# Weights' second parts made by transfers that add, in place of a VectorE subtraction, with four slots of each kind

## The chip, the core and the metric

The program runs on one core of one Trainium2 chip. The metric is the device time of one execution, in microseconds (us), and lower is better. The kernel before took 3535.98 us (median of two runs, 3535.84 and 3536.11).

## The reference

The reference is a chain of two transformer stacks on 512 tokens of width 1024, all in fp32. The first has four layers; each projects the normalised tokens (w_in, 1024 x 3328), mixes them (stick-breaking attention in layers 0 and 3, differential attention in layer 1, a short convolution in layer 2), adds an attention over 256 memory tokens (w_mem_kv), projects back (w_o) and runs a gated feed-forward of inner width 2816 (w_ffn_in, w_ffn_out). The second has one layer: a spatial gating branch and an RWKV-7 recurrence side by side, then a feed-forward of inner width 4096. Nearly all arithmetic is a product of tokens with weights:

```
proj = hn @ w_in[i]
x = x + jnp.concatenate([mix, mo], axis=-1) @ w_o[i]
gu = x @ w_in;  (silu(gu[..., :D_FF]) * gu[..., D_FF:]) @ w_out
p = a @ w_in[l];  h = h + mixed @ w_out[l]
h = h + jnp.square(jax.nn.relu(f @ w_ffn1[l])) @ w_ffn2[l]
```

## The kernel before, in words

Tokens lie along the free axis and features along the 128 partitions. To keep fp32 accuracy at the speed of the format fp32r, every operand of a large product is split into two fp32r parts, `hi` (the value rounded) and `lo` (what the rounding left). A product is then three matmuls: hi times hi, hi times lo, lo times hi (`mm3`).

Weights come in chunks of 128 x 1024 fp32 (512 KB), made by `wblk`. For each chunk:

1. SyncE loads the raw weights into a slot of the ring `wr` (line 305).
2. ScalarE casts them into a slot of the ring `wh`, the hi part.
3. VectorE subtracts wh from wr into a slot of the ring `wl`, the lo part (`sub`).
4. TensorE runs 24 matmuls of 512 columns (or 48 of 256) on wh and wl, which frees both slots.

There are 584 chunks, some 8 of them smaller than 512 KB. The rings have `WR` and `WH` slots; before, three each. A new chunk's cast can run when TensorE has done with the chunk three before it. The instructions of `wblk` have a raised priority (`WPRI`), so the scheduler of the framework puts them into each engine's order ahead of other ready work. Each engine then executes its own order strictly in sequence, so an instruction that waits holds up all that stand behind it on that engine. GpSimd (POOL) has few instructions in this kernel: it issues the transfers that aren't weight loads, such as `mx` (memory tokens, loaded back from DRAM at the end of each mixing stage by `mem_load`), and in the second stack `ar`, `bk`, `dL`, `dv`, `bv`, `gl`, `dga`, `dob` (stored) and `W`, `vv`, `x`, `c` (loaded) for the recurrence.

All other temporaries of 128 x 512 fp32 (`c`) come from one pool: `NCT` slots in the first stack, `NCT2` in the second. The recurrence (`chain`) is a side lane of eight rounds, between whose matmuls the planner puts those of weights (`ga`, `gb`, and `acc` of w_pa). Every recorded compute instruction and POOL transfer carries the line 152, that of the wrapper which records it; matmuls carry line 285.

Of the kernel before, what the change touches and what calls it, by code (L numbers as in the profile page):

```python
# [8 lines left out]
F32 = mybir.dt.float32  # L9
F32R = mybir.dt.float32r  # L10
AF = mybir.ActivationFunctionType
ALU = mybir.AluOpType
# [160 lines left out]
class Build:  # L173
# [123 lines left out]
    def wblk(self, src, kc, cols, also={}, sizes=None):  # L297

        nc = self.nc
        step = max(1, 1024 // cols)  # L300
        out, k0, rows = [], 0, src.shape[0]
        with self.tc.high_priority(offset=WPRI):
            for i, n in enumerate(sizes or [min(step, kc - k) for k in range(0, kc, step)]):
                raw = self.wp.tile([rows, n, cols], F32, tag="wr", name=self.nm("wr"), bufs=WR)
                nc.sync.dma_start(out=raw, in_=src[:, k0:k0 + n])
                also.get(i, lambda: 0)()
                hi = self.wp.tile([rows, n, cols], F32R, tag="wh", name=self.nm("wh"), bufs=WH)
                lo = self.wp.tile([rows, n, cols], F32R, tag="wl", name=self.nm("wl"), bufs=WH)
                self.untimed |= {hi.name, lo.name}
                nc.scalar.copy(hi, raw)  # L310
                self.sub(lo, raw, hi)
                out += [(hi[:, k], lo[:, k]) for k in range(n)]
                k0 += n
        return out
# [790 lines left out]
    def pools2(self, ctx):  # L1105
        ep = ctx.enter_context
        self.kp = ep(self.tc.tile_pool(name="kp2", bufs=NCT2, reuse_waits="tile"))
        self.sp = ep(self.tc.tile_pool(name="sp2", bufs=4, reuse_waits="tile"))
# [690 lines left out]
MW, DW, M0, FILL, MS = 1, 1.5, 8, (99, 1, 99), 8  # L1799
VL, KSU, ENDS = 2, "kkksksss", 1  # L1800
SPRI, SOLVE_LAT, KSL, ZSL = 200, 1.3, 2, 6
NCT2 = 31
LRL, ZB, HOLD, CY, END = 0.6, 2, 2, 0.1, 2
WR, WH, WPRI, NCT = 3, 3, 150, 37


def program(tc, nc, out, depth=DEPTH, second=True, **io):
# [40 lines left out]
```

## Time and profile before

| what | value |
|---|---|
| median of the runs | 3535.98 us |
| the profiled execution's own time | 3537.37 us |
| its span, first to last instruction | 3535.6 us |
| TensorE matmul busy | 3497.0 us (99%) |
| VectorE busy | 1930.7 us (55%) |
| ScalarE busy | 1431.8 us (40%) |
| GpSimd busy | 201.9 us (6%) |
| weight loads (queue q1) | 306.22 MB, 27.3% of 16 DMA engines |
| GpSimd's transfers (queue q0) | 68.67 MB, 7.2% |

PE is TensorE's matmul row and PEld its weight load, which overlaps it; DVE is VectorE, ACT ScalarE, POOL GpSimd, SP SyncE. A letter q behind an engine means its queue of issues. The matmuls' durations overlap because they are pipelined, so a rate is read from a count over a stretch of time and not from a mean. DMA share is the mean busy share of the core's 16 DMA engines.

### The profile page before, as it was taken

Reading aid. Unit: us, or ns where it says so; the run is one execution under the profiler, and the core shown is the slowest. Engines: PE = TensorE matmul, PEld = TensorE weight load, DVE = VectorE, ACT = ScalarE, POOL = GpSimd, SP = SyncE. Lnnn points to the kernel's source line nnn. Section 1 sums busy time; section 2 is a strip of 40 time slices with the busy share of each in tenths; the row PEclk is TensorE's granted clock in tenths of the full one; section 3 lists DMA queues with packets and bytes.
Section 4 is the critical chain, followed back from the end, with each engine's and each line's share of the span. In section 5 each row is a group of like instructions: output and inputs, shape, how many; then the busy total and the mean of one; then the engine's idle time right before and its main releaser. Section 6 shows DMA issues by size and latency. Waiting matters only on the chain. (4 is left out here: it accounts for less than half of the span.)

```text
span 3535.6 us, 43485 instructions
## 1 busy us (share of the span) xinstructions
PE 3497.0 (99%) x17462; PEld 2941.1 (83%) x17462; DVE 1930.7 (55%) x2879; ACT 1431.8 (40%) x2198; POOL 201.9 (6%) x315
## 2 busy tenths in 40 slices
PE   9999999999999999999999999999999999999998
PEld 7888888888888888888888888888878888788887
DVE  7675444577643456553446665444687645464434
ACT  6673222444432343332235663223564433443322
POOL 1000000000000000000000000000033332200000
PEclk9999999999999999999999999999999999999999
DMA  5232333323333233323332122333366665433332
GB/s 186 80 96 96 94 99 97 96 72 99 99 95 99 95 96 108 107 96 95 101 95 84 60 72 96 95 101 96 111 191 161 153 190 144 153 96 99 98 95 78
DMA packets 116139, 377.81 MB, mean 107 GB/s; under 512 B 14544, under 2 KB 23184, under 8 KB 115936
## 3 DMA queue, kind: packets, MB, share of 16 engines
q1 hardware_dynamic: 94112, 306.22, 27.3%
q0 software_dynamic: 21680, 68.67, 7.2%
q8 instruction: 137, 2.24, 0.3%
q14 instruction: 66, 0.54, 0.0%
q10 hardware_dynamic: 144, 0.13, 0.0%
HBM read 344.00 MB, written 30.93 MB: 106 GB/s over the span
## 5 line engine op out<-in xcount | busy, mean ns | idle before, releaser
L152 DVE TENSOR_TENSOR wl<-wr,wh 128x1024 fp32r<-128x1024 f32 (+2 forms) x584 | 702.5, 1205 | 929.7 <-ACT wh L152 922.7
L152 ACT CAST wh<-wr 128x1024 fp32r<-128x1024 f32 (+2 forms) x584 | 604.8, 1038 | 1210.4 <-PE acc L285 536.5
L285 PE MATMUL g<-xl,wh 128*128 128x512 f32 x704 | 273.9, 389 | 0.0
L285 PE MATMUL g<-xh,wh 128*128 128x512 f32 x704 | 273.9, 389 | 0.0
L285 PE MATMUL acc<-hid,wl 128*128 128x512 f32 x704 | 273.9, 389 | 0.0
L285 PE MATMUL u<-xh,wl 128*128 128x512 f32 x704 | 273.9, 389 | 0.0
L285 PE MATMUL u<-xh,wh 128*128 128x512 f32 x704 | 273.9, 389 | 0.0
L285 PE MATMUL u<-xl,wh 128*128 128x512 f32 x704 | 273.9, 389 | 0.0
L285 PE MATMUL acc<-hid,wh 128*128 128x512 f32 x704 | 273.9, 389 | 0.0
L285 PE MATMUL acc<-hidl,wh 128*128 128x512 f32 x704 | 273.9, 389 | 0.0
L285 PE MATMUL g<-xh,wl 128*128 128x512 f32 x704 | 273.8, 389 | 0.0
L152 ACT ACTIVATE c<-c 128x512 f32<-128x512 f32 (+1 forms) x163 | 102.3, 629 | 269.6 <-DVE c L152 268.8
L285 PE MATMUL qk<-xh,wh 128*128 128x512 f32 x448 | 180.3, 402 | 6.6 <-ACT xh L152 6.6
L285 PE MATMUL acc<-h,wh 128*128 128x512 f32 x448 | 173.3, 395 | 4.8 <-ACT h L152 3.7
L285 PE MATMUL acc<-hl,wh 128*128 128x512 f32 x448 | 176.4, 394 | 0.6 <-DVE hl L152 0.5
L285 PE MATMUL qk<-xl,wh 128*128 128x512 f32 x448 | 176.1, 393 | 0.5 <-DVE xl L152 0.5
L285 PE MATMUL qk<-xh,wl 128*128 128x512 f32 x448 | 175.8, 392 | 0.0
L285 PE MATMUL acc<-h,wl 128*128 128x512 f32 x448 | 175.4, 392 | 0.0
L285 PEld LDWEIGHTS g<-xh,wl 128*128 128x128 f32 x704 | 132.2, 188 | 27.6
L285 PEld LDWEIGHTS acc<-hidl,wh 128*128 128x128 f32 x704 | 132.1, 188 | 27.5
L285 PEld LDWEIGHTS g<-xl,wh 128*128 128x128 f32 x704 | 132.1, 188 | 27.5
L285 PEld LDWEIGHTS u<-xh,wh 128*128 128x128 f32 x704 | 132.2, 188 | 27.4
(445 smaller groups left out, 7445.0 us busy)
## 6 DMA issues: line engine op xcount, KB each, us to landing
wr<-in_w_fi SPq DMA_DIRECT2D x176, 512.0 KB, 3.7
wr<-in_w_in SPq DMA_DIRECT2D x103, 512.0 KB, 3.8
wr<-in_w_fo SPq DMA_DIRECT2D x80, 512.0 KB, 3.5
wr<-in_w_f SPq DMA_DIRECT2D x64, 512.0 KB, 3.7
wr<-in_w SPq DMA_DIRECT2D x58, 512.0 KB, 4.4
wr<-in_w_o SPq DMA_DIRECT2D x40, 512.0 KB, 3.6
wr<-in_w_kv SPq DMA_DIRECT2D x16, 512.0 KB, 3.8
mx<-dmh POOLq DMA_DIRECT2D x16, 256.0 KB, 6.0
```

The source lines that it names most:

```text
L152: r = f(*a, **k)
L285: self.nc.tensor.matmul(out, lhsT, rhs, start=start, stop=stop, **kw)
```

## The change

ScalarE now makes, after the cast, a second tile: minus the hi part, written into the slot of `wl`. GpSimd then issues a transfer within SBUF that adds the raw weights onto that tile, so `wl` holds raw minus hi as before. VectorE's subtraction is gone from `wblk` (it stays for all other splits). The rings have four slots of each kind in place of three, and to make room the pool `c` has 32 slots in place of 37 in the first stack and 25 in place of 31 in the second.

```diff
                 nc.scalar.copy(hi, raw)
-                self.sub(lo, raw, hi)
+                nc.scalar.activation(out=lo, in_=hi.bitcast(F32), func=AF.Copy, scale=-1.0)
+                nc.gpsimd.dma_start(out=lo, in_=raw, accum_op=ALU.add)
...
-NCT2 = 31
+NCT2 = 25
...
-WR, WH, WPRI, NCT = 3, 3, 150, 37
+WR, WH, WPRI, NCT = 4, 4, 150, 32
```

The new instructions move the order of others. On ScalarE, in layer 0's last attention heads (`uh`, `V`, `q`, `t` are the heads' own tiles), before:

```order
L152 CAST wh_2263<-wr_2261 128x1024
L152 CAST uh_2013<-t_1955 128x512
L152 COPY mix_2011<-o_1998 128x512
L152 CAST uh_2013<-t_1955 128x512
L152 CAST uh_2013<-t_1955 128x256
L152 CAST V_2026<-t_1955 128x384
```

and now:

```order
L152 CAST wh_2269<-wr_2267 128x1024
L152 CAST uh_2024<-t_1982 128x512
L152 CAST uh_2024<-t_1982 128x256
L152 ACTIVATE wl_2270<-wh_2269 128x1024
L152 CAST V_2037<-t_1982 128x384
L152 CAST V_2041<-t_1982 128x256
```

The negation (ACTIVATE wl) stands a few instructions behind its cast, with other work between.

On POOL, at the end of layer 1's mixing (`mx` are the eight loads of memory tokens, `c<-in_bias` the last head's bias), before:

```order
L152 DMA c_6781<-in_bias 128x512
L152 DMA mx_7177<-dmh 128x512
L152 DMA mx_7179<-dml 128x512
L152 DMA mx_7181<-dmh 128x512
L152 DMA mx_7183<-dml 128x512
L152 DMA mx_7185<-dmh 128x512
L152 DMA mx_7187<-dml 128x512
L152 DMA mx_7189<-dmh 128x512
L152 DMA mx_7191<-dml 128x512
L152 DMA c_7284<-in_bias 128x512
```

and now:

```order
L152 DMA wl_7545<-wr_7542 128x1024
L152 DMA mx_7327<-dmh 128x512
...
L152 DMA mx_7341<-dml 128x512
L152 DMA wl_7552<-wr_7549 128x1024
L152 DMA c_7399<-in_bias 128x512
L152 DMA wl_7563<-wr_7560 128x1024
L152 DMA wl_7615<-wr_7612 128x1024
L152 DMA wl_7689<-wr_7686 128x1024
```

A chunk's adding transfer (wl) now stands behind all eight loads, and others behind the bias.

On POOL, in one round of the second stack's recurrence, before:

```order
L152 DMA dob<-c_22896 1024x1x64
L152 DMA x_22392<-dL 64x8x64
L152 DMA c_22960<-bv 128x512
L152 DMA c_22961<-gl 128x512
L152 DMA vv_23056<-dv 64x2x512 x2
L152 DMA x_22392<-dL 64x8x64
L152 DMA bk_23054<-bk 128x1024
L152 DMA W_23239<-ar 64x1024 x2
```

and now:

```order
L152 DMA dob<-c_23445 1024x1x64
L152 DMA wl_23643<-wr_23640 128x1024
L152 DMA wl_23650<-wr_23647 128x1024
L152 DMA c_23509<-bv 128x512
L152 DMA c_23510<-gl 128x512
L152 DMA bk_23585<-bk 128x1024
L152 DMA W_23586<-ar 64x1024 x2
L152 DMA vv_23587<-dv 64x2x512 x2
```

Two adding transfers now stand ahead of the loads of the round's operands.

## Rows read from the trace of the kernel before

**Rows 1.** The page's first part: busy us, share of the span, instructions.
```profile
PE 3497.0 (99%) x17462; PEld 2941.1 (83%) x17462; DVE 1930.7 (55%) x2879; ACT 1431.8 (40%) x2198; POOL 201.9 (6%) x315
```

**Rows 2.** Busy time by stretch: stretch, us, busy by engine, PEclk, DMA share, GB/s.
```profile
1000.00:1300.00 300.00, 300.00 (x1325) 248.43 (x1324) 130.13 (x155) 89.19 (x107) 0.00 (x0) 1.00 0.31 97
2500.00:2600.00 100.00, 97.65 (x606) 84.67 (x604) 72.84 (x106) 67.15 (x112) 16.30 (x24) 1.00 0.50 161
2600.00:2700.00 100.00, 98.97 (x606) 78.83 (x605) 75.42 (x116) 58.57 (x96) 44.70 (x60) 1.00 0.71 175
2700.00:2850.00 150.00, 146.02 (x739) 123.38 (x738) 106.44 (x167) 55.25 (x77) 50.07 (x72) 0.97 0.60 155
```

**Rows 3.** The same stretches, of wl's instructions alone: PE, PEld, DVE.
```profile
1000.00:1300.00 300.00, 171.67 (x442) 82.77 (x441) 67.37 (x57) 1.00 0.31 97
2500.00:2600.00 100.00, 63.93 (x200) 37.26 (x199) 22.73 (x20) 1.00 0.50 161
2600.00:2700.00 100.00, 44.01 (x111) 20.96 (x112) 17.10 (x14) 1.00 0.71 175
2700.00:2850.00 150.00, 64.27 (x165) 30.99 (x165) 25.48 (x21) 0.97 0.60 155
```

**Rows 4.** Waits of TensorE on weights: us in total, times, longest.
```profile
PE acc L285 <- ACT wh L152: 1.7, 2, 1.1
PE k L285 <- ACT wh L152: 0.9, 1, 0.9
PE v L285 <- DVE wl L152: 0.7, 1, 0.7
PE vm L285 <- DVE wl L152: 0.2, 1, 0.2
```

**Rows 5.** Groups of instructions: busy us, mean ns of one, idle before, releasers.
```profile
L152 DVE TENSOR_TENSOR wl<-wr,wh 128x1024 fp32r<-128x1024 f32 (+2 forms) x584 | 702.5, 1205 | 929.7 <-ACT wh L152 922.7 <-PE ms L285 4.2
L152 ACT CAST wh<-wr 128x1024 fp32r<-128x1024 f32 (+2 forms) x584 | 604.8, 1038 | 1210.4 <-PE acc L285 536.5 <-PE u L285 361.3 <-issue 60.6
L152 ACT ACTIVATE c<-c 128x512 f32<-128x512 f32 (+1 forms) x163 | 102.3, 629 | 269.6 <-DVE c L152 268.8
L152 ACT CAST hid<-c 128x512 fp32r<-128x512 f32 x88 | 55.0, 625 | 54.5 <-DVE c L152 54.5
```

**Rows 6.** DMA queues (packets, MB, share) and issues (KB each, median us to landing).
```profile
q1 hardware_dynamic: 94112, 306.22, 27.3%
q0 software_dynamic: 21680, 68.67, 7.2%
...
wr<-in_w_fi SPq DMA_DIRECT2D x176, 512.0 KB, 3.7
...
X<-dL POOLq DMA_DIRECT2D x2, 512.0 KB, 10.5
```

**Rows 7.** POOL's issues of mx: ns min, median, max; first and last start.
```profile
L152 POOL DMA_DIRECT2D mx<-dmh x16: 539/539/544, 64.3 to 1356.5; - x16
```

**Rows 8.** Timeline of VectorE at the start: start us, us, idle before.
```profile
5.49 0.42 DVE L152 TENSOR_TENSOR wl<-wr,wh 128x256 fp32r<-128x256 f32 x1
...
8.58 0.96 DVE L152 TENSOR_TENSOR wl<-wr,wh 128x768 fp32r<-128x768 f32 x1 [0.46 <-ACT wh L152]
```

**Rows 9.** Timeline of TensorE at the start.
```profile
15.76 0.50 PE L285 MATMUL qk<-xh,wh 128*128 128x512 f32 x1 [0.46 <-ACT xh L152]
```

**Rows 10.** Timeline of POOL at layer 1's loads of mx, and at a round.
```profile
811.01 0.54 POOL L152 DMA_DIRECT2D mx<-dmh  x1 [51.33 <-PE dn L285]
...
828.09 0.54 POOL L152 DMA_DIRECT2D mx<-dml  x1
829.88 0.54 POOL L152 DMA_DIRECT2D c<-in_bias  x1 [1.25 <-DVE aTl L152]
...
2989.67 1.07 POOL L152 DMA_DIRECT2D W<-ar  x2 [2.60 <-PE B L285]
```

**Rows 11.** Busy time by stretch at the recurrence's end (columns as in rows 2).
```profile
3030.00:3050.00 20.00, 18.11 (x105) 15.69 (x106) 10.53 (x22) 8.14 (x15) 4.12 (x7) 0.91 0.31 92
```

## The prediction

> **What bounds the kernel now.** I read the page's first part, the busy time by stretch, the waits of TensorE, the groups of instructions, the DMA part, and last the timelines at the places where something might give way. TensorE is busy for 3497.0 of 3535.6 us [rows 1], so all idle time together is 38.6 us, 1.1% of the span. No change that leaves the matmuls alone can win more, and this change leaves their number and shapes alone. In the feed-forward there is no idle time at all: 300.00 of 300.00 us [rows 2]. The subtraction that is removed is no bound: VectorE does 584 of them in 702.5 us, but of the time it idles before them 922.7 us goes to waiting for the cast, and the cast in turn waits for TensorE to free a slot (536.5 and 361.3 us are the largest shares) [rows 5]. TensorE itself waited for a weight part for only 1.7 + 0.9 + 0.7 + 0.2 = 3.5 us [rows 4]. So the question is not what VectorE gains, but whether the longer way to `wl` stays hidden.
>
> **How much cover there is.** A full chunk is 24 matmuls of 512 columns. In 300 us 1325 matmuls run [rows 2], so one takes 0.226 us and a chunk 5.43 us. With three slots a freed slot has two ready chunks ahead of it, 10.9 us of TensorE; with four it has three, 16.3 us.
>
> **The change part by part.**
>
> *VectorE* loses 702.5 us. It hides beside TensorE, so I count zero. If VectorE had been late somewhere, the 38.6 us bound the gain.
>
> *ScalarE* gains 584 negations of 128 x 1024. No such row exists; at 128 x 512 an ACTIVATE takes 629 ns and a CAST 625 [rows 5], so a negation costs about a cast, 1.04 us, 607 us in all. ScalarE goes from 1431.8 [rows 1] to some 2040 us, 58%. It has room everywhere: in its fullest stretch it goes from 67 to about 88 of 100 us (20 chunks [rows 2, 3]).
>
> *POOL* gains 584 issues. Its plain issues take 0.54 us [rows 7], 315 us together: 5% of what it could do.
>
> *The adding transfer.* No row shows one. Below, it can't be shorter than a weight load of the same 512 KB in the same rows, 3.7 us to landing; above, the slowest 512 KB on POOL's queue, with very short runs, took 10.5 us [rows 6]. For what it takes of the DMA engines: 57 chunks in 300 us at a share of 0.31 [rows 2, 3] make 93 / 57 = 1.63 us of all 16 engines for a load. The adding transfer must read two tiles, source and destination, and write one, so I take two loads, 3.26 us; the bounds are one load (1.63) and, from the landing of 10.5, about 8. For the landing I take 3.7 + 1.63 and some queueing behind loads, 6.0 us. This is the weakest term. The Trainium skill, Collectives: The Full Stack, section The bandwidth ceiling, says of the add inside a DMA engine that it costs two source reads and not the addition, and measures about 31 GB/s per engine for a copy and half for a reduction. By that the transfer would take an estimated 2.1 us of 16 engines (1 MiB read at 16 x 31 GB/s), and the DMA terms below would vanish; no run here shows it yet.
>
> *The way to wl.* Before: cast 1.04, subtraction 1.20, some 0.3 of handing over: 2.5 of 10.9 us, 8.4 us spare. Now: cast 1.04, negation 1.04, issue 0.54, landing 6.0: 8.6 of 16.3 us, 7.7 us spare. The spare is nearly the same, so in steady work TensorE should notice nothing, and the 3.5 us of waits stays about as it is. It holds up to a landing of 13.7 us. The load of a raw chunk now waits for the adding transfer; it has a slot more and TensorE's 5.4 us a chunk besides, so it hides too.
>
> *The DMA engines.* In the feed-forward each 5.26 us (300 / 57) now has 1.63 + 3.26 = 4.89 us of DMA work: a share of 0.93. It fits, barely. In the second stack's middle it does not: 2500 to 2600 goes from 0.50 by 20 x 3.26 us to 1.15; 2600 to 2700 from 0.71 by 14 to 1.17; 2700 to 2850 from 0.60 by 21 to 1.06 [rows 2, 3]. That is 15 + 17 + 9 = 41 us too much. The rings swallow their spare of 7.7 us in each of the three: **+18 us**. At one load it is zero.
>
> *The start.* The first two second parts were ready at 5.9 and 9.5 us [rows 8]. They now need a negation and a transfer in place of a subtraction, some 4 to 6 us more. TensorE waits for tokens again at 15.76 [rows 9] anyhow, and that hides a part: **+4 us**.
>
> *POOL's order.* An adding transfer behind a POOL transfer that waits is late. At layer 1's end the eight mx loads, some 4.3 us of issues, were spread over 811.0 to 828.6 us, because each waits for a free `c` slot, and the bias follows at 829.9 [rows 10]; with five slots fewer this won't be shorter. One chunk's transfer stands right behind them: 13.3 us late, less 7.7 spare: **+6 us**. The same loads in layers 0 and 2 took less than the spare in excess, so I count nothing there.
>
> **Sum.** 18 + 4 + 6 = 28 us over the profiled execution's 3537.37, 3565; the median of the runs is 1.4 us below that execution, so I predict **3564 us**, +0.8%, within the 2% (71 us) that counts here as no change.
>
> **The rivals.**
>
> *The adding transfer is dear, and the DMA engines become the bound (slower).* In the feed-forward there are 5.26 - 1.63 = 3.6 us for it; from 2.2 loads on, every chunk is late. At three loads the DMA work is 584 x 6.52 = 3808 us and 255 us of POOL's other transfers (7.2% [rows 6] of the span): **4060 us**; at 2.5 loads it is 5.71 - 5.26 = 0.45 us a chunk, 263 us over all 584, about 3800. A landing above 13.7 us does the same by way of the rings: each us more costs a quarter of a us per chunk, 146 us. For it speaks that no row shows an addition in a transfer, so nothing in the trace excludes the upper bound; against it, that two reads and one write of the same bytes need no more than two loads. The Trainium skill, DMA: Bandwidth & Descriptors, section Issuing engines are not separate DMA queues, says that transfers of all queues run on the same 16 engines and interleave; the shares that add up in rows 2 show why that matters here.
>
> *POOL's order delays the recurrence (slower).* In each of eight rounds the loads of the operands now stand behind two adding transfers, which wait for TensorE to free a slot. Around the last rounds TensorE is busy for 18.1 of 20 us [rows 11], so the planner has little left to put in between, and the recurrence's own waits decide. A round that comes 10 us later costs up to 80 us: about **3630 us**; with what I counted it decides from 5 us a round. Against it: the rounds' operands are loaded a round ahead, and POOL already waits there without harm (2.60 us before W [rows 10]).
>
> *It hides wholly (no change).* With a transfer of one load's price, the four slots cover the rest, and the 3.5 us of waits on weights go: about **3530 us**. A gain beyond 38.6 us is excluded.
>
> **How the numbers follow.** My forecast has a chance of 0.55, the dear transfer 0.25, the delayed recurrence 0.12 (0.10 of it above 2%), the hidden one 0.08. Faster by over 2% needs what the idle time doesn't hold: I leave 0.02 for a mechanism that I don't see, out of the forecast's share. Slower is 0.25 + 0.10 = 0.35, and within 2% the rest, 0.63. The range begins at 3525, a little below the hidden case, and reaches to 3800: it takes in the delayed recurrence and the dear transfer up to some 2.5 loads, and leaves out its upper part, about 0.15. The forecast's own range is 3530 to 3600.
>
> **What would show it.** Right: TensorE still at 300 of 300 us between 1000 and 1300; VectorE near 1230 us and ScalarE near 2040; DMA shares near 0.9 in the feed-forward; a landing of 5 to 8 us; waits of TensorE on wl's transfers at the start, near layer 1's end and between 2500 and 2850 only. Wrong: a DMA share at 1 or a landing above 13 us in the feed-forward, with TensorE waiting there for each chunk; or rounds of the recurrence further apart than before, with POOL waiting on a weight transfer ahead of W and vv. If the DMA share stays near 0.6, the transfer costs less than I took and the 18 us is too much.

## The result, and the profile after

The changed kernel took 3649.30 us (median of two runs, 3644.38 to 3654.22) against 3535.98 us: a ratio of 1.032, 95% interval 1.026 to 1.038. It is slower by 113 us, 3.2%, where 3564 us and no measurable change were forecast. The time lies in the range given; the likeliest case was the wrong one. The profiled execution took 3644.38 us with a span of 3642.6, and its rows are set against the span before, 3535.6 us: a difference of 107 us.

The page's first part of the changed kernel, which answers to [rows 1]:

```profile
PE 3536.7 (97%) x17462; PEld 2965.5 (81%) x17462; DVE 1275.6 (35%) x2295; ACT 1997.6 (55%) x2781; POOL 700.6 (19%) x899
```

The matmuls are as many, yet TensorE is idle for 3642.6 - 3536.7 = 105.9 us where it was idle for 38.6, and it is busy for 39.7 us more. So 67 of the 107 us are waiting and 40 are matmuls that take longer. VectorE lost 655 us and gained the kernel nothing.

The stretches of [rows 2], in the changed kernel (stretch, us, busy time of PE, PEld, DVE, ACT, POOL, granted clock, DMA share, GB/s):

```profile
1000.00:1300.00 300.00, 300.00 (x1325) 248.41 (x1324) 65.36 (x95) 142.06 (x159) 47.62 (x57) 1.00 0.84 192
2500.00:2600.00 100.00, 95.99 (x602) 83.92 (x600) 48.25 (x81) 74.52 (x118) 21.10 (x28) 1.00 0.82 200
2600.00:2700.00 100.00, 85.97 (x460) 64.60 (x461) 56.43 (x91) 66.41 (x92) 44.69 (x61) 0.91 0.88 213
2700.00:2850.00 150.00, 136.47 (x644) 112.14 (x643) 80.05 (x144) 75.69 (x107) 60.64 (x73) 0.92 0.94 219
```

The feed-forward is untouched: 300.00 of 300.00 us at a DMA share of 0.84. Between 2600 and 2850 us TensorE is busy for 222.4 us where it was for 245.0, at a granted clock of 0.91 and 0.92 in place of 1.00 and 0.97, while the DMA share went from 0.71 and 0.60 to 0.88 and 0.94. (The work has moved some 29 us to the right by then, so the stretches hold nearly, not wholly, the same work.)

Where in the program the time went is read from the first and last start of a tile's matmuls. Of TensorE's instructions by tile, before (count, ns of one as min/median/max, first to last start in us, form; `g` is the first stack's feed-forward, `acc<-hid` its second half, `G` the recurrence, `f` the second stack's feed-forward):

```profile
L285 PE MATMUL g<-xh,wh x704: 389/389/397, 302.4 to 2436.4; 128*128 128x512 f32 x176
L285 PE MATMUL acc<-hid,wh x704: 389/389/389, 422.5 to 2499.0; 128*128 128x512 f32 x176
L285 PE MATMUL G<-W,bk x256: 272/272/373, 2857.0 to 3029.7; 64*128 64x128 f32 x128
L285 PE MATMUL f<-xh,wh x256: 389/389/397, 3172.8 to 3466.4; 128*128 128x512 f32 x128
```

and in the changed kernel:

```profile
L285 PE MATMUL g<-xh,wh x704: 389/389/397, 321.9 to 2465.5; 128*128 128x512 f32 x176
L285 PE MATMUL acc<-hid,wh x704: 389/389/389, 442.0 to 2528.1; 128*128 128x512 f32 x176
L285 PE MATMUL G<-W,bk x256: 272/272/579, 2937.3 to 3130.3; 64*128 64x128 f32 x128
L285 PE MATMUL f<-xh,wh x256: 389/389/397, 3278.9 to 3572.5; 128*128 128x512 f32 x128
```

Read as differences: 19.5 us are lost by layer 0's first feed-forward matmul, 29.1 by the first stack's last one, 80.3 by the recurrence, 106.1 by the second feed-forward. `f` itself lasts 293.6 us in both. So the second stack's middle, from `acc<-hid`'s last to `f`'s first start, costs 750.8 us where it cost 673.8: **+77 us**; the first stack costs 29, two thirds of it at the start; the feed-forwards nothing.

Groups of instructions and DMA issues of the changed kernel, which answer to [rows 5] and [rows 6] (for the issues: KB each, median us to landing):

```profile
L152 ACT ACTIVATE wl<-wh 128x1024 fp32r<-128x1024 f32 (+2 forms) x584 | 608.3, 1044 | 12.7
L152 POOL DMA_DIRECT2D wl<-wr x584 | 497.6, 856 | 2652.4 <-ACT wl L152 2387.5
...
q0 software_dynamic: 105744, 369.65, 52.4%
q1 hardware_dynamic: 94112, 306.22, 26.6%
...
wl<-wr POOLq DMA_DIRECT2D x564, 512.0 KB, 5.9
wr<-in_w_fi SPq DMA_DIRECT2D x176, 512.0 KB, 5.1
```

The negation takes 1.04 us and the adding transfer lands in 5.9 us, both as forecast. From the queue: (0.524 x 3642.6 - 0.072 x 3535.6) us for 300.98 MB, as much as 574 full chunks, makes 2.88 us of all 16 engines for one. A load of weights now lands in 5.1 us, not 3.7.

### The profile page after: what moved, and what is told of

The parts are those of the page before. It is cut to its first block, busy times and chain, and to the rows that moved or that the text cites. A ratio compares the mean times of both kernels' runs of the same rounds, so it can differ in the third digit from the quotient of the medians.

```text
span 3642.6 us, 44823 instructions
## 1 busy us (share of the span) xinstructions
PE 3536.7 (97%) x17462; PEld 2965.5 (81%) x17462; DVE 1275.6 (35%) x2295; ACT 1997.6 (55%) x2781; POOL 700.6 (19%) x899
## 4 chain that ended last, share of the span: by engine, by line
PE 85%; DMA 6%; issue 3%; ACT 3%; DVE 1%; POOL 1%; SPq 0%; DVEq 0%; POOLq 0%; ACTq 0%
PE acc L285 27%; PE g L285 13%; PE u L285 13%; PE qk L285 8%; PE f L285 5%; PE v L285 4%; PE cv L285 2%; DMA wl<-wr 2%; PE gb L285 1%; PE z L285 1%; PE G L285 1%; PE B L285 1%; PE su L285 1%; ACT wl L152 1%; PE o L285 1%
## 5 line engine op out<-in xcount | busy, mean ns | idle before, releaser
L152 POOL DMA_DIRECT2D wl<-wr x584 | 497.6, 856 | 2652.4 <-ACT wl L152 2387.5
L152 ACT ACTIVATE wl<-wh 128x1024 fp32r<-128x1024 f32 (+2 forms) x584 | 608.3, 1044 | 12.7
L152 DVE TENSOR_TENSOR x<-x,acc 128x512 f32<-128x512 f32 x136 | 92.3, 685 | 651.3 <-PE acc L285 651.3
L152 DVE TENSOR_TENSOR c<-g,R 128x512 f32<-128x512 f32 x88 | 60.8, 691 | 409.3 <-PE g L285 408.8
L285 PE MATMUL acc<-h,wh 128*128 128x512 f32 x448 | 177.8, 404 | 14.6 <-ACT h L152 14.6
```

The lines of the kernel that those rows point to most:

```text
L152: r = f(*a, **k)
L285: self.nc.tensor.matmul(out, lhsT, rhs, start=start, stop=stop, **kw)
```

## The experiments

Each is set against the kernel before; "second stack" is the time from `acc<-hid`'s last to `f`'s first start, whole and up to the first `G`, from each profile's tile rows.

| kernel | median us | ratio (95%) | first `g` | last `acc<-hid` | second stack (to `G`) |
|---|---|---|---|---|---|
| before | 3535.98 | | 302.4 | 2499.0 | 673.8 (358.0) |
| changed | 3649.30 | 1.0321 (1.0261-1.0380) | 321.9 | 2528.1 | 750.8 (409.2) |
| slots | 3563.94 | 1.0076 (1.0061-1.0091) | 299.0 | 2495.2 | 699.0 (381.7) |
| act_add | 3589.69 | 1.0151 (1.0136-1.0166) | 302.9 | 2507.6 | 716.8 (389.5) |
| spare_add | 3623.77 | 1.0249 (1.0232-1.0266) | 309.8 | 2517.8 | 737.9 (410.2) |
| transfer | 3688.65 | 1.0436 (1.0418-1.0454) | 320.0 | 2575.1 | 746.8 (415.2) |
| pool25 | 3540.17 | 1.0008 (0.9999-1.0017) | 303.4 | 2500.0 | 675.4 (362.4) |
| plan | 3566.76 | 1.0081 (1.0066-1.0096) | 300.6 | 2498.7 | 702.3 (381.5) |
| spare_copy | 3583.95 | 1.0132 (1.0117-1.0147) | 305.3 | 2511.7 | 707.9 (385.9) |
| spare_sp2 | 3622.09 | 1.0231 (1.0213-1.0249) | 305.4 | 2517.2 | 750.3 (418.8) |
| told | 3620.20 | 1.0237 (1.0221-1.0252) | 321.9 | 2526.4 | 728.7 (398.6) |
| first_told | 3567.73 | 1.0091 (1.0076-1.0106) | 321.8 | 2531.4 | 674.1 (360.7) |
| ffn_told | 3536.43 | 1.0001 (0.9991-1.0010) | 299.3 | 2496.2 | 673.6 (360.5) |
| late | 3613.61 | 1.0217 (1.0200-1.0234) | 299.1 | 2503.3 | 748.7 (405.9) |

A profile is one execution. That of slots took 3559.69 us, 4 below its median, and that of spare_sp2 3632.71, 11 above; so the last three columns are good to some us only, and they don't add up to the medians exactly.

"The planner is told" means this: every recorded instruction calls `note`, which adds an estimate of its cost to that engine's busy time, and the planner decides by these estimates how long a side lane stands back and what goes between. An instruction issued around the recording wrapper can be told as another one.

**slots: the change without its transfer.** VectorE subtracts again; the rings of four and the smaller pools stay, and the planner is told of the negation and the transfer.

```diff
-                nc.scalar.activation(out=lo, in_=hi.bitcast(F32), func=AF.Copy, scale=-1.0)
-                nc.gpsimd.dma_start(out=lo, in_=raw, accum_op=ALU.add)
+                self.nc.nc.vector.tensor_tensor(out=lo, in0=raw, in1=hi.bitcast(F32), op=ALU.subtract)
+                self.note("A", "activation", lo, [hi], {})
+                self.note("G", "dma_start", lo, [raw], {})
```

> The changed kernel's rings of four and its smaller pools, with VectorE's subtraction put back in place of the negation and the adding transfer; the planner is told the same loads as in the changed kernel, so its order stays that of the change. Theory A (the adding transfers fill the DMA engines and delay the other transfers of the second stack and the start): all of the loss is gone, 3536 to 3550 us. Rival B (the smaller pools and the order that the planner makes for them): most of the loss stays, 3590 us or more. Rival C (ScalarE's extra work) and rival D (POOL's order, in which adding transfers wait and hold up others) say the same here as A: 3536 to 3550.

3563.94 us, between the two times expected. A quarter of the loss is there without any of the new work, and all of it in the second stack (699.0 for 673.8 us); the first stack is 4 us shorter.

**pool25 and plan: which part of that.** The kernel before with `NCT2 = 25` alone, and the kernel before with nothing but the telling (its own rings and pools, and VectorE's subtraction, told as in slots):

```diff
-NCT2 = 31
+NCT2 = 25
```

> The kernel before, with one number changed: the second stack's pool of temporaries has 25 slots in place of 31. The run with the slots alone lost 27 us, all in the second stack. If the smaller pool is the cause: 3555 to 3565 us here. If it is the order that the planner makes when it believes ScalarE and POOL to be busier: 3534 to 3542.

```diff
-                self.sub(lo, raw, hi)
+                self.nc.nc.vector.tensor_tensor(out=lo, in0=raw, in1=hi.bitcast(F32), op=ALU.subtract)
+                self.note("A", "activation", lo, [hi], {})
+                self.note("G", "dma_start", lo, [raw], {})
```

> The kernel before with its rings of three and pools of 37 and 31 and its subtraction, but the planner is told of a ScalarE instruction and a POOL transfer per chunk in place of a VectorE one, as in the changed kernel. If the planner's order is the cause of the 27 us: 3555 to 3565 us. If the smaller pool is: 3534 to 3542.

3540.17 and 3566.76 us. The pool is worth nothing; the telling alone costs 31 us. In plan the chip does the same work as before, in another order only, and loses 28.5 us in the second stack. So it is the order that the planner makes when it counts 584 issues on POOL and negations on ScalarE. TensorE's largest wait in plan's second stack is that of `acc` for its activations `h`, behind the recurrence's last rounds: 12.0 us where it was 3.7. At 14.6 us it is also the largest of the changed kernel. From the last `G` to `f` plan takes 143.5 us with that wait in it, and before it was 143.1; so matmuls that stood there now stand ahead of it. The wait before, in plan and in the changed kernel (in total, times, longest):

```profile
PE acc L285 <- ACT h L152: 3.7, 3, 1.8
```

```profile
PE acc L285 <- ACT h L152: 12.0, 3, 7.8
```

```profile
PE acc L285 <- ACT h L152: 14.6, 4, 8.2
```

**act_add: ScalarE's part.** The negation stays, VectorE adds in place of the transfer; the planner is told as in the change.

```diff
-                nc.gpsimd.dma_start(out=lo, in_=raw, accum_op=ALU.add)
+                nc.nc.vector.tensor_tensor(out=lo, in0=lo.bitcast(F32), in1=raw, op=ALU.add)
+                self.note("G", "dma_start", lo, [raw], {})
```

> As the changed kernel, but the raw weights are added onto the negated first part by VectorE and not by a transfer. ScalarE has all its new work, POOL and the DMA engines have none. Theory A and rival D: 3540 to 3555 us. Rival C (ScalarE's extra 608 us): 3590 us or more. Rival B: 3590 or more, as in the run with the slots alone.

3589.69 us, 26 over slots: 12 in the first stack, 18 in the second. ScalarE is busy for 1997.4 us, as in the change. Of the 18 us, 9 are waiting (36 us of idle time for 27) and 9 are longer matmuls. TensorE's waits that end with a ScalarE instruction come to 27.7 us there, in slots to 21.2; those for weights to 1.0. So ScalarE's 56% of the span hides that it stands between TensorE and its activations there.

**spare_add, spare_copy, spare_sp2: the DMA engines' part.** VectorE subtracts, and beside it each full chunk is sent into one of two spare tiles that nothing reads: by POOL with the addition, by POOL as a plain copy, and by SyncE as two plain copies. `wr` has four slots, `wh` and `wl` three. (The chunk's slot of `wr` is held until the transfer has read it, and the next transfer into the same spare tile waits for it, with what stands behind that one on the issuing queue; TensorE waits for none.)

```diff
...
+                self.turn = 1 - self.turn
+                if rows == P:
+                    nc.nc.gpsimd.dma_start(out=self.spare[self.turn][:, :n * cols], in_=raw.rearrange("p n c -> p (n c)"), accum_op=ALU.add)
...
```

> VectorE's subtraction is back and makes the second part; beside it POOL adds each raw chunk onto one of two spare tiles that nothing reads (wr has four slots, wh and wl three, the spare tiles take the rest of the room). So the DMA engines and POOL carry the same bytes, but TensorE waits for none of them, and POOL's transfers wait for the raw load alone and not for ScalarE and TensorE. Theory A: most of the loss is back, 3590 to 3640 us, with the second stack's stretch some 50 us longer and DMA shares as in the changed kernel. Rival D (POOL waiting for ScalarE's negation, and TensorE for the transfer): little of it, 3540 to 3565 us.

spare_copy and spare_sp2 are shown against spare_add:

```diff
-                    nc.nc.gpsimd.dma_start(out=self.spare[self.turn][:, :n * cols], in_=raw.rearrange("p n c -> p (n c)"), accum_op=ALU.add)
+                    nc.nc.gpsimd.dma_start(out=self.spare[self.turn][:, :n * cols], in_=raw.rearrange("p n c -> p (n c)"))
```

> As the run with the adding transfers onto spare tiles, but each is a plain copy: the same number of POOL transfers, the same bytes written, half the bytes read. If the DMA engines' work is what delays the second stack, the 60 us over the run with the slots alone shrink to some 20 to 35: 3585 to 3600 us, and the feed-forward's DMA share goes from about 0.84 to about 0.6. If POOL's queue is (more issues in front of the second stack's transfers), nothing changes: 3615 to 3630.

```diff
-                self.turn = 1 - self.turn
...
-                    nc.nc.gpsimd.dma_start(out=self.spare[self.turn][:, :n * cols], in_=raw.rearrange("p n c -> p (n c)"), accum_op=ALU.add)
+                    for t in self.spare:
+                        nc.nc.sync.dma_start(out=t[:, :n * cols], in_=raw.rearrange("p n c -> p (n c)"))
```

> As the run with adding transfers onto spare tiles, but SyncE issues two plain copies of each chunk onto the spare tiles in their place: the DMA engines read the same bytes, POOL has only its old transfers. Loads stand behind copies on SyncE, which may cost a little of its own. If the DMA engines are the cause: 3605 to 3640 us. If POOL's queue is: 3560 to 3580.

3623.77, 3583.95 and 3622.09 us: 60, 20 and 58 over slots. Stretches of slots, of spare_copy, of spare_add and of spare_sp2 (columns as above), in that order:

```profile
2600.00:2700.00 100.00, 91.08 (x555) 72.82 (x554) 71.64 (x111) 54.63 (x90) 38.57 (x53) 0.93 0.60 155
```

```profile
1000.00:1300.00 300.00, 300.00 (x1325) 248.48 (x1325) 125.80 (x148) 84.95 (x100) 30.20 (x57) 1.00 0.57 192
2600.00:2700.00 100.00, 90.74 (x535) 71.88 (x534) 70.34 (x106) 59.37 (x85) 40.62 (x64) 0.97 0.83 240
```

```profile
1000.00:1300.00 300.00, 300.00 (x1325) 248.43 (x1324) 126.02 (x148) 85.38 (x101) 48.17 (x57) 1.00 0.83 192
2600.00:2700.00 100.00, 84.95 (x449) 66.11 (x448) 64.79 (x96) 51.95 (x74) 43.56 (x62) 0.86 0.87 211
```

```profile
1000.00:1300.00 300.00, 300.00 (x1326) 248.39 (x1325) 128.22 (x152) 87.58 (x106) 0.00 (x0) 1.00 0.81 284
2600.00:2700.00 100.00, 86.95 (x443) 66.38 (x443) 65.35 (x97) 51.27 (x73) 32.59 (x48) 0.83 0.94 300
```

Two plain copies on SyncE's queue make the DMA share of one adding transfer on POOL's (0.81 and 0.83) and, by the medians, the same loss. Neither the addition nor POOL's queue is needed for it. POOL waits nearly as long to issue a copy as an adding transfer, 229 and 256 us in the second stack, yet one copy costs 9 us there and the adding transfer 39. What is left is the time that the 16 engines spend, and the loss is not in proportion to it. In the feed-forward all of them are free, at 300.00 us busy.

Neither comparison is clean by itself: an adding transfer also takes POOL longer to issue (0.858 for 0.535 us), and in spare_sp2 SyncE's loads stand behind the copies, so part of its loss may be its own: its longest wait is for a `wl` of VectorE. First that line, then the largest waits of spare_add between 2517 and 2930 us (in total, times, longest):

```profile
PE r L285 <- DVE wl L311: 13.1, 1, 13.1
```

```profile
PE ss L285 <- ACT c L152: 8.2, 3, 4.9
PE ZT L285 <- ACT c L152: 6.8, 1, 6.8
PE sv L285 <- DVE rc L152: 3.3, 1, 3.3
```

These are intermediate values of the recurrence's preparation (`ss`, `ZT`) and of the spatial gating branch (`sv`); of the 52 us that TensorE waits in spare_add's second stack only 3 are for weights.

What the busier DMA engines do to others is seen at the recurrence's operands. Landing of the transfers of `bk` between 2500 and 2990 us, first before, then the changed kernel:

```profile
DMA to landing us min/median/max: 3.4/4.8/11.8
```

```profile
DMA to landing us min/median/max: 3.4/8.0/12.9
```

The medians are 4.3 us in slots, 5.6 in spare_copy, 7.4 in spare_add and 9.0 in spare_sp2, where the copies are in SyncE's queue and not in that of `bk`; so standing behind weight transfers in POOL's queue is not needed for it.

The four largest of TensorE's waits between 2528 and 2940 us in the changed kernel (in total, times, longest):

```profile
PE gl L285 <- DVE bk L152: 6.3, 2, 4.8
PE r L285 <- DMA wl<-wr: 5.8, 1, 5.8
PE r L285 <- ACT wh L152: 4.4, 1, 4.4
PE ss L285 <- ACT c L152: 3.7, 2, 2.2
```

Only two of these four are for weights, and of the 56 us that TensorE waits in the whole second stack 16 are. In the whole run it waits 24.4 us for transfers of `wl`, under a quarter of its idle time.

**transfer: the change without its four slots.**

```diff
-NCT2 = 25
+NCT2 = 31
-WR, WH, WPRI, NCT = 4, 4, 150, 32
+WR, WH, WPRI, NCT = 3, 3, 150, 37
```

> The change with the old sizes: negation and adding transfer, but rings of three, and pools of 37 and 31 slots. The way to the second part is about 8.9 us (1.04 cast, 1.04 negation, 0.6 issue, 5.9 landing, 0.3 handing over) of the 10.9 us that two chunks cover. Theory A: the second stack loses as in the changed kernel, and the feed-forward begins to wait here and there: 3640 to 3720 us. Rival B (smaller pools): clearly faster than the changed kernel, 3600 or less. Rival D: as A, since less cover makes more waits.

3688.65 us: the change with four slots is 39 us faster, and all of that is gained in the first stack, whose end comes at 2575.1 us here and at 2528.1 there; the second stack is 4 us shorter here. (The pools differ as well; that of the second stack was worth nothing in pool25.) By the prediction's arithmetic the way to `wl` (8.6 us) leaves 2.3 of 10.9 us with three slots, which any burst uses up: even the stretch from 1000 to 1300 us has TensorE busy for 298.87 us only.

**told, first_told, ffn_told, late: the parts put together.** told is the change, with the planner told in the second stack of the subtraction of before; first_told moreover subtracts there in truth; ffn_told uses the transfer for the 320 chunks of the feed-forwards alone; late is the change with subtractions until layer 0's output projection.

```diff
...
+                if self.block == 0:
+                    self.note("A", "activation", lo, [hi], {})
+                    self.note("G", "dma_start", lo, [raw], {})
+                else:
+                    self.note("V", "tensor_tensor", lo, [raw, hi], {})
```

> The changed kernel with one thing undone: in the second stack the planner is told of a VectorE subtraction per chunk, as before, though negation and adding transfer are still issued (in the first stack it is told as in the change, and the pools stay at 32 and 25). If the order that the planner makes costs its 27 us here as it did alone: 3615 to 3630 us. If that order matters only where the DMA engines are free, and their work hides it: 3640 or more. If the order of before is worse with late second parts: above 3655.

```diff
+                if self.block == 0:
+                    nc.nc.scalar.activation(out=lo, in_=hi.bitcast(F32), func=AF.Copy, scale=-1.0)
+                    nc.nc.gpsimd.dma_start(out=lo, in_=raw, accum_op=ALU.add)
+                else:
+                    self.nc.nc.vector.tensor_tensor(out=lo, in0=raw, in1=hi.bitcast(F32), op=ALU.subtract)
...
```

> Negation and adding transfer in the first stack alone; the second stack subtracts on VectorE and is planned as before. If the second stack's loss comes from the DMA engines' work and the planner's order there, and the first stack's 29 us from its own start and mixing stages: 3560 to 3575 us, with the first stack ending some 29 us later than before and the second as long as before.

```diff
-                w = self.wblk(io["w_fi"][l, c], NC_, 256)
+                w = self.wblk(io["w_fi"][l, c], NC_, 256, adds=True)
...
```

> Negation and adding transfer for the feed-forward's chunks alone, in both stacks, 320 of 584; all others by VectorE's subtraction; the second stack planned as before; four slots, pools of 32 and 25. If the transfers cost nothing where only weights move, and all that was lost was lost beside other transfers and at the start: 3530 to 3545 us, within the measurement of the kernel before. If the transfers cost TensorE something in the feed-forward too: 3555 or more.

```diff
...
+                if self.late:
+                    nc.scalar.activation(out=lo, in_=hi.bitcast(F32), func=AF.Copy, scale=-1.0)
+                    nc.gpsimd.dma_start(out=lo, in_=raw, accum_op=ALU.add)
+                else:
+                    self.nc.nc.vector.tensor_tensor(out=lo, in0=raw, in1=hi.bitcast(F32), op=ALU.subtract)
...
```

> The changed kernel, but until layer 0's projection back (w_o) the second parts are made by VectorE's subtraction; the planner is told as in the change. The changed kernel reached layer 0's feed-forward 19.5 us later than before, the run with the slots alone 3.4 us earlier. If the longer way to the second part is what the start loses by, where the rings have no lead yet: 3620 to 3632 us, with layer 0's feed-forward beginning at 297 to 304 us. If the start loses by the pool or the order there: 3640 or more.

told gets 29 us back, first_told 82, ffn_told all 113, late 36 (3613.61 us, 6 less than the least expected, with the first `g` where it was expected). In the second stack told is 54.6 us over first_told (728.7 and 674.1). That is what negation and transfers cost there with the order of before, and it is near the 57 us of act_add's 18 and spare_add's 39. In ffn_told more than half of the adding transfers run, at nearly the changed kernel's DMA share, and cost nothing:

```profile
1000.00:1300.00 300.00, 300.00 (x1325) 248.56 (x1324) 71.44 (x101) 140.53 (x159) 43.95 (x52) 1.00 0.81 189
3300.00:3400.00 100.00, 100.00 (x443) 82.87 (x442) 15.80 (x23) 49.28 (x57) 15.20 (x18) 1.00 0.87 196
```

No version beats the kernel before: the best is level with it.

## Why the prediction was wrong, point by point

**Right: steady work.** The way to `wl` is 1.04 + 1.04 + 0.85 + 5.9 = 8.8 us, forecast as 8.6, and the rings cover it: TensorE stays at 300 of 300 us. VectorE came to 1275.6 us (near 1230 forecast) and ScalarE to 1997.6 (2040); the landing to 5.9 us (6.0); the feed-forward's share to 0.84 (0.93). That VectorE's work was worth nothing is shown by ffn_told, which is level with the kernel before although VectorE is busy for 1551.6 us in place of 1930.7. That the time fell into the range is luck: the range reached to 3800 us for a dear transfer and a delayed recurrence, and neither came as it was described. (A slip: 315 us of issues on POOL are 9% of the span, not 5; at 0.856 us each they came to 497.6.)

**Failed: the DMA engines, +18 us in the second stack.** The transfer was priced well, 2.88 us of 16 engines for 3.26. What failed is the rule of the sum: only what a share has over 1 was counted, less the spare of the weight rings. With 2.88 us a chunk the rule gives shares of 1.08, 1.11 and 1.00 in the three stretches, 19 us too much, of which the rings' spare leaves 4. From `acc<-hid`'s last to `f`'s first start the work even fits: 0.55 x 673.8 us and 88 chunks of 2.88 are 624 us of 673.8. Yet spare_add lost 39 us over slots there, at a share of 0.83. That stretch before, in spare_add and in the changed kernel (columns as above):

```profile
2499.00:3172.80 673.80, 659.61 (x3860) 552.69 (x3859) 428.39 (x676) 314.47 (x500) 172.75 (x259) 0.98 0.55 153
```

```profile
2517.80:3255.70 737.90, 686.16 (x3861) 572.04 (x3860) 430.78 (x676) 315.78 (x500) 251.08 (x346) 0.94 0.83 201
```

```profile
2528.10:3278.90 750.80, 694.74 (x3861) 572.53 (x3859) 332.54 (x588) 400.18 (x589) 252.41 (x347) 0.94 0.81 197
```

The engines need not be full: `bk` lands after 8.0 us in place of 4.8, and what the recurrence's preparation loads and stores one after the other has no ring ahead of it. The rings' spare was taken for work that doesn't go through the rings. The dear transfer, the rival with a chance of 0.25, named the resource; its price of 2.5 or 3 loads and its place, every chunk, did not come.

By the bandwidth rule of the Trainium skill, Collectives: The Full Stack, section The bandwidth ceiling, an addition costs two source reads and so half the rate. The trace agrees: one copy in spare_copy takes (0.307 x 3582.6 - 0.071 x 3557.9) us / 573 chunks = 1.48 us of 16 engines, one adding transfer in spare_add (0.532 x 3619.5 - 0.071 x 3557.9) / 573 = 2.92, 1.97 times as much. The estimate of 2.1 us that the prediction made from that page's 31 GB/s was too low by over a quarter, and that the DMA terms would then vanish was wrong too: the plain copy, at 1.48 us, still costs 9 us.

**Failed: "it has room everywhere", of ScalarE.** Counted at nothing, it costs 26 us (act_add over slots), 18 of them in the second stack. A share of a stretch says that the work fits; it doesn't say that it may stand ahead of what TensorE needs next, and the negation, recorded in `wblk`, has `wblk`'s raised priority. (Another priority for it was not tried.)

**Not counted: the planner's order.** 27 to 31 us (slots and plan over before), 25 to 28 in the second stack. The prediction took the order of before for the second stack, and looked at POOL's order only as a queue.

**Not counted: matmuls that take longer.** The sum held TensorE's busy time at 3497.0 us, because the matmuls are the same. It grew by 39.7 us, 35 of them in the rows above (659.61 to 694.74), at a granted clock of 0.94 in place of 0.98.

**Failed in size: the start, +4 us.** The first two second parts were ready for TensorE at 12.93 and 17.54 us in the changed kernel's timeline, some 7 and 8 us later than in [rows 8] (4 to 6 forecast):

```profile
12.93 0.79 PE L285 MATMUL qk<-xh,wl 128*128 128x512 f32 x1 [3.71 <-DMA wl<-wr]
...
17.54 0.50 PE L285 MATMUL qk<-xh,wl 128*128 128x512 f32 x1 [1.68 <-DMA wl<-wr]
```

And it did not end with two chunks. TensorE's waits from 0 to 330 us in the changed kernel:

```profile
PE qk L285 <- ACT xh L152: 6.8, 1, 6.8
PE ms L285 <- DVE c L152: 6.4, 1, 6.4
PE qk L285 <- DMA wl<-wr: 5.4, 2, 3.7
PE v L285 <- DMA wl<-wr: 5.2, 1, 5.2
PE vm L285 <- DMA wl<-wr: 1.7, 2, 1.3
```

Waits on `wl`'s transfers come to 12.3 us, that of `ms` was 0.6 before. By `g` the kernel is 19.5 us behind; late, which subtracts up to there, is 22.8 us ahead of the change (299.1). Not all of it is the way to `wl`: spare_add, whose transfers TensorE waits for nowhere, reaches `g` 10.8 us after slots, act_add 3.9. The other 9.6 us of the first stack are lost behind `g`; TensorE waits at the ends of the mixing stages there, 3.3 us for an `h` and 5.1 for `mix` (7.0 us for that `h` in spare_add, 5.7 for `mix` in act_add).

**Did not come: POOL's order, +6 us.** In POOL's timeline of the changed kernel the eight loads of `mx` at layer 1's end, spread from 811.0 to 828.6 us in [rows 10], are issued without long gaps, the last at 860.07:

```profile
860.07 0.54 POOL L152 DMA_DIRECT2D mx<-dml  x1 [1.10 <-DMA mx<-dmh]
...
860.99 0.89 POOL L152 DMA_DIRECT2D wl<-wr  x1 [0.37 <-ACT wl L152]
```

**The second rival, POOL's order in the recurrence,** gave 3630 us and came nearest by number, for the wrong reason. The matmuls of `G` last 193.0 us for 172.7, so the rounds cost 20 us, not 80; the larger loss, 51 us, is ahead of the first round, in the preparation.

**The sum.** For the second stack slots gives 25, spare_add 39 and act_add 18 us over their bases: 82 for the 77 measured. With the 29 us of the first stack, 25 of which late takes back, that makes 111 for the 107 us of the profiled execution. told bears out the planner's part (22 us less than the change in the second stack) and the other two together (55). Open is how these two share in the change itself: no run has the transfer on the way to `wl` without the negation ahead of it. Open too is how much of the 40 us of longer matmuls is the lower clock.

## What to carry to other kernels

Before giving work to the DMA engines, ask which transfers have no ring of slots ahead of them: here a stage that loads and stores in a chain paid for a DMA share of 0.83, while a stage that only streams weights paid nothing at 0.87. Where an order is planned from noted costs, an edit that changes what is noted is also an edit of the order; the cheapest experiment is the old work told as the new. Deeper rings cover a longer way to an operand in steady work but not at the start, where no slot is full yet: the first `g` comes at 320.0 us with three slots (transfer) and at 321.9 with four.

## What the runs showed of the hardware

- A transfer within SBUF that adds takes 1.97 times the DMA engine time of a plain copy of the same 512 KB (2.92 and 1.48 us of 16 engines), and lands in 5.7 us where the copy lands in 3.4 (medians of spare_add and spare_copy).
- It is also dearer to issue. Groups of POOL, in spare_copy and then in spare_add: 0.535 us for a copy, 0.858 with the addition.

```profile
L316 POOL DMA_DIRECT2D spare<-wr x583 | 311.1, 535 | 2767.4 <-DMA wr<-in_w_fi 821.7
```

```profile
L316 POOL DMA_DIRECT2D spare<-wr x583 | 496.8, 858 | 2634.7 <-DMA wr<-in_w_fi 723.1
```

- The clock fell where TensorE was made to wait: 0.91 between 2600 and 2700 us, a mean between the levels of 1.2 and 2.4 GHz, in a stretch with 14.0 us of idle time; before, with 1.0 us idle, it was at 1.00. With it came 40 us of longer busy time for the same 17462 matmuls; that this is the clock was not tried by itself.
